# Layer 0's opening of a two-layer decoder trunk: where its subtractions run, how wide its w_ada multiply-adds are, and how many column blocks it begins

## The chip, the cores and the metric

The kernel runs on one core of a Trainium2 chip, with one launch. The metric is the device time of one execution in microseconds (us); lower is better. The core has five engines with a queue of their own each: TensorE (PE; its weight loads are listed apart as PEld), VectorE (DVE), ScalarE (ACT), GpSimd (POOL) and SyncE (SP), which here only issues transfers. An engine takes its instructions strictly in the order in which the program lists them, and waits on semaphores for the others. 16 DMA engines carry the transfers from HBM.

## What is computed

Two layers of a decoder. Each layer modulates its normalised input by vectors that come from c, projects it once into all heads and gates of three attention branches, merges them and adds to the residual. x has 256 rows of 2048 float32; w_in has 17944 columns per layer. What matters here is the start of layer 0:

```python
for l in range(2):
    mod = silu(c) @ w_ada[l] + b_ada[l]            # c: (1, 2048), w_ada[l]: (2048, 6144)
    shift, scale, gate = split(mod, 3)
    h = rmsnorm(x, norm_pre_g[l]) * (1 + scale) + shift
    a_q, a_k, a_v, a_z, ..., m_g = split(h @ w_in[l])   # w_in[l]: (2048, 17944)
    ...                                            # three attentions, w_branch, gates, w_out, residual
```

No column of h is known before the columns of shift and scale that belong to it. These need a full pass over 2048 rows of w_ada.

## The kernel before

**Products.** A float32 product is made of three products of a rounded type: a weight tile `raw` of 128x1024 (two k-tiles of 128 rows by 512 columns, 512 KB) is split by `split` (L265) into `wh`, a rounded copy made by ScalarE (L272), and `wl = raw - wh` (L273), made by VectorE unless an engine is passed. Likewise h is kept as `hh` and `hl`. `mm3` (L276) then runs `hh*wh`, `hh*wl`, `hl*wh` (L277 to L279). Below, a **unit** is one such weight tile: 2 k-tiles x 2 halves of 128 rows of x x 3 products = 12 matmuls of 512 columns, one cast and one subtraction. A column block of w_in (512 columns) has 8 units, over the 16 k-tiles of h.

**The body of the kernel** is `run_jobs` (L359): a list of jobs, one for each column block, unit after unit. Casts and subtractions run three units ahead (`L_CAST`), and loads four tiles ahead. Attention steps, evacuations (`sc.urgent`, one each tick) and the background multiply-adds of the next modulation vectors (`ada_steps`, L434) are woven between the units.

**Layer 0's opening** is `start_layer0` (L899). Nothing of h is there at the start, so it computes shift and scale in pieces and begins column blocks of w_in with those k-tiles of h that are ready:

- w_ada's columns for shift and scale are taken in 8 chunks of 2 k-tiles (256 columns of shift and 256 of scale). A chunk needs all 2048 rows: 8 tiles of 512 KB, which are loaded in two transfers each. For each tile VectorE runs two multiply-adds (`madd`, L238: L240 the first one, L242 the others) of 128x512 into two accumulators.
- When a chunk is complete, `colsums` (L938) adds the two accumulators (L939), lets TensorE sum over the partitions (`colsum`, L246, behind the transposes of x, L516), finishes the columns (L251, L253) and writes these two k-tiles of hh and hl (L525 on VectorE, L527 and L533 on ScalarE, L534 on VectorE). It is queued one item after the chunk's last tile (`CLAG`).
- Between a chunk's w_ada tiles lie units of w_in, spread evenly (`seq`). `PLAN` says which: the blocks 0 to 3 (`LO`), 4 to 7 (`HI`) and block 8, each in segments of one to three units. In all there are 59 units in the opening. Their subtraction is passed to GpSimd (`split(w, NW, nc.gpsimd)`).
- A unit's matmuls are queued 3 items after it (`MLAG`). A segment holds two of the four PSUM banks; 6 items after its last unit (`SPILL`) it is stored by ScalarE (L965, a block's first segment) or added by VectorE into the block's partial result (L967).
- Raw tiles have 7 buffers (`RAW_BUFS`), wh and wl 4 each (`W_BUFS`). Transfers are issued by SP in the order of `seq`, 6 tiles ahead. x (two transfers of 1 MB) is issued ahead of all w_ada.
- x is normalised by ScalarE (`norm_x`, L501: L506, L510) ahead of its first cast.

After the opening the blocks begun in it are finished as ordinary jobs over their remaining k-tiles, the rest is added to the partial result (L1034). The jobs run in the order of layer 0's program: branch A's q, k, v, z (first half), four blocks of the merge gate, branch A's second half, and so on. In the kernel before, the merge gate blocks are `LO`, branch A's first four are `HI`, and block 8 is the first of branch A's second half.

Of the kernel before, what the change touches and what calls it, by code (L numbers as in the profile page):

```python
# [11 lines left out]
F32 = mybir.dt.float32  # L12
# [5 lines left out]
P = 128  # L18
# [65 lines left out]
def tiles(r, k0, k1):  # L84
    return [(i, k0, k1) for i in r]


LO, HI = range(4), range(4, 8)
PLAN = [tiles(LO, 0, 1), tiles(HI, 0, 2) + [(8, 0, 2)], tiles(LO, 1, 3), tiles(HI, 2, 4) + [(8, 2, 4)], tiles(LO, 3, 5), tiles(HI, 4, 6),
        tiles(LO, 5, 7) + [(8, 4, 7)]]  # L90
RAW_BUFS = 7
# [4 lines left out]
def body(ctx, tc, a, out):  # L96
# [51 lines left out]
    for f in vec_loads(0, nc.scalar):  # L148
        f()
    for t in range(NT):  # L150
        nc.sync.dma_start(xs[:, t], x_dram[0][t])

# [746 lines left out]
    def start_layer0(hh, hl, w_in, cols, parts, plan, mcols, S_):  # L899
        wv = a["w_ada"][0].rearrange("(k p) n -> p k n", p=P)  # L900
        CW = 2 * P
        NP = KD // 2
        seq = []
        done_k = [0] * len(cols)
        for p in range(NP):
            ws = [(i, k) for i, ks in plan[p] for k in ks]
            assert all(k < p for _, k in ws)
# [6 lines left out]
        raws, banks, accs = {}, {}, {}  # L914
        events = {}
        state = [0]

        def load_next():
            n = state[0]
            if n < len(seq):  # L920
                kind, x, y = seq[n]
                r = raw_tile()
                if kind == "a":
                    v = r.rearrange("p (k h n) -> p k h n", k=2, h=2)
                    for h in range(2):
                        c0 = h * D + x * CW
# [5 lines left out]
                raws[n] = r.rearrange("p (k n) -> p k n", k=2)  # L932
                state[0] += 1
# [3 lines left out]

        def colsums(p):  # L938
            nc.vector.tensor_add(accs[p][0], accs[p][0], accs[p][1])  # L939
            g = h_chunks(lambda k, t: xs[:, t, k * P:(k + 1) * P], p, lambda: (hh, hl), mcols[0], mcols[1])  # L940
            next(g)
            pb = pbank()
            for i in range(4):
                colsum(pb, i, [accs[p][0][:, i * P:(i + 1) * P]])
            for third in range(2):
                finish_cols(0, third, mcols[third], pb[:, 2 * third:2 * third + 2], 2 * p, 2)
            for _ in g:
                pass

# [23 lines left out]
        norm_x(xs, ssx, parts[7].rearrange("p t n -> p (t n)"))  # L973
        S_["lam"] = {}
# [6 lines left out]
        for n, (kind, x, y) in enumerate(seq):  # L981
            w = raws.pop(n)
            if kind == "a":
                if y == 0:
# [22 lines left out]
    def layer(l, S_, jobs):  # L1007
# [34 lines left out]
        if l == 0:  # L1042
            begin()
            first = [C_MG + j * NW for j in range(4)] + [C_AQ, C_AK, C_AV, C_AZ, C_AQ + NW, C_AK + NW]
            gpv = big.tile([P, D], F32, tag="gp", name="gpv", bufs=1).rearrange("p (j t n) -> p j t n", j=2, t=NT)
            qv = qk_tile().rearrange("p j s -> p (j s)").rearrange("p (t n) -> p t n", t=NT)
            ys = [big.tile([P, NT, NW], F32, tag=g, name="yv", bufs=2) for g in ("yh", "yl")]
            parts = [gpv[:, 0], gpv[:, 1], qv] + [pj() for _ in range(5)] + ys
            plan = [[]] + [[(i, list(range(k0, k1))) for i, k0, k1 in p] for p in PLAN]
# [449 lines left out]
```

## Time and profile before

| | us |
|---|---|
| time, median of 3 runs | 2314.87 (2314.47 to 2317.6) |
| span of the profiled execution | 2310.3 |
| TensorE busy in the span | 2223.7 |
| VectorE busy | 1561.6 |
| ScalarE busy | 1011.0 |
| GpSimd busy | 248.7 |

The profile gives for its one execution the span from the first to the last instruction; that is 4.6 us less than the median of the timed runs. Busy times are the time in which an engine has an instruction in work. Matmuls are pipelined, so a busy TensorE may still be waiting a little; the granted clock (PEclk, 1.00 is 2.4 GHz, 0.50 is 1.2 GHz) is read beside it. Rows of a timeline merge neighbouring instructions of one kind ("x4") and give start, length and, in brackets, the idle time ahead of them and what ended it.

### The profile page before, as it was taken

What the parts mean: (1) busy time and instruction counts of PE and PEld (TensorE: products, weight loads), DVE (VectorE), ACT (ScalarE), POOL (GpSimd) and SP (SyncE); (2) the same over time, 40 slices, a digit from 0 to 9 for tenths busy, and PEclk for the clock granted to TensorE, in tenths of its full rate; (3) what the DMA queues carried; (4) which work ended last, traced back from release to release, by engine and by line L of the source; (5) the groups of instructions that cost most, each with busy time, mean ns of one, the idle gap of its engine ahead of it and who ended that gap; (6) DMA issues with size and microseconds to landing.
All of it is one profiled execution on the core that took longest, in us unless ns stands there. A gap on an engine that the chain in (4) does not pass through costs nothing.

```text
span 2310.3 us, 30428 instructions
## 1 busy us (share of the span) xinstructions
PE 2223.7 (96%) x11474; PEld 1891.4 (82%) x11474; DVE 1561.6 (68%) x1991; ACT 1011.0 (44%) x1429; POOL 248.7 (11%) x170
## 2 busy tenths in 40 slices
PE   5787899999999999999999999999999999999998
PEld 3666788999988889888877888889998888987886
DVE  7999897767677757677556655565556564666664
ACT  4332355444444435454445444444444443445443
POOL 4765400000001100001110000000000010000010
PEclk9988999999999999999999999999999999999999
DMA  9877777887878877667656677667666776655663
GB/s 312 272 235 252 243 238 233 253 260 219 248 229 263 262 230 253 197 199 246 219 168 192 190 217 220 192 189 214 183 204 180 218 219 199 206 175 164 195 232 121
DMA packets 317603, 504.76 MB, mean 218 GB/s; under 512 B 16921, under 2 KB 124177, under 8 KB 317201
## 3 DMA queue, kind: packets, MB, share of 16 engines
q1 hardware_dynamic: 317232, 502.54, 69.8%
q8 instruction: 90, 1.47, 0.3%
q14 instruction: 57, 0.46, 0.1%
q10 hardware_dynamic: 224, 0.29, 0.0%
HBM read 498.56 MB, written 4.19 MB: 218 GB/s over the span
## 4 chain that ended last, share of the span: by engine, by line
PE 87%; DVE 7%; issue 3%; DMA 1%; ACT 1%; SPq 0%; POOL 0%; DVEq 0%; ACTq 0%; POOLq 0%
PE mbank L277 22%; PE mbank L279 22%; PE mbank L278 22%; DVE wk L242 5%; PE mbank L422 4%; PE mbank L423 4%; PE mbank L424 4%; DMA raw<-w_ada 1%; PE pbank L756 1%; DVE wk L240 1%; PE pbank L628 1%; PE pbank L878 1%; PE pbank L851 1%; PE pbank L583 1%; PE pbank L246 0%
## 5 line engine op out<-in xcount | busy, mean ns | idle before, releaser
L273 DVE TENSOR_TENSOR wl<-raw,wh 128x1024 fp32r<-128x1024 f32 (+1 forms) x668 | 809.8, 1217 | 586.7 <-ACT wh L272 582.6
L272 ACT CAST wh<-raw 128x1024 fp32r<-128x1024 f32 (+1 forms) x730 | 751.1, 1033 | 762.5 <-PE mbank L279 539.3
L277 PE MATMUL mbank<-wh,hh 128*128 128x512 f32 (+1 forms) x1912 | 764.9, 400 | 17.8 <-DVE gpv L967 6.9
L278 PE MATMUL mbank<-wl,hh 128*128 128x512 f32 (+1 forms) x1912 | 740.5, 387 | 7.1 <-POOL wl L273 6.7
L279 PE MATMUL mbank<-wh,hl 128*128 128x512 f32 (+1 forms) x1912 | 739.8, 387 | 0.0
L277 PEld LDWEIGHTS mbank<-wh,hh 128*128 128x128 f32 x1912 | 364.6, 191 | 93.6 <-issue 14.8
L278 PEld LDWEIGHTS mbank<-wl,hh 128*128 128x128 f32 x1912 | 364.8, 191 | 80.8 <-POOL wl L273 9.3
L279 PEld LDWEIGHTS mbank<-wh,hl 128*128 128x128 f32 x1912 | 363.6, 190 | 75.2 <-DVE hl L534 0.9
L422 PE MATMUL mbank<-hh,wh 128*128 128x256 f32 x768 | 220.2, 287 | 0.0
L424 PE MATMUL mbank<-hh,wl 128*128 128x256 f32 x768 | 217.3, 283 | 0.0
L423 PE MATMUL mbank<-hl,wh 128*128 128x256 f32 x768 | 217.2, 283 | 0.0
L242 DVE SCALAR_TENSOR_TENSOR acc<-raw,cT,acc 128x512 f32<-128x512 f32 x240 | 185.6, 773 | 5.9 <-DMA raw<-w_ada 1.4
L273 POOL TENSOR_TENSOR wl<-raw,wh 128x1024 fp32r<-128x1024 f32 x62 | 161.9, 2630 | 94.5 <-ACT wh L272 57.1
L242 DVE SCALAR_TENSOR_TENSOR wk<-raw,cT,wk 128x512 f32<-128x512 f32 x112 | 167.8, 1557 | 1.9 <-DMA raw<-w_ada 1.9
L277 PE MATMUL mbank<-wh,yh 128*128 128x512 f32 x384 | 150.6, 392 | 0.0
L279 PE MATMUL mbank<-wh,yl 128*128 128x512 f32 x384 | 149.6, 390 | 0.0
L278 PE MATMUL mbank<-wl,yh 128*128 128x512 f32 x384 | 149.5, 389 | 0.0
L423 PEld LDWEIGHTS mbank<-hl,wh 128*128 128x128 f32 x768 | 147.3, 192 | 0.5
L422 PEld LDWEIGHTS mbank<-hh,wh 128*128 128x128 f32 x768 | 147.2, 192 | 0.5
L424 PEld LDWEIGHTS mbank<-hh,wl 128*128 128x128 f32 x768 | 147.2, 192 | 0.0
L1153 POOL TENSOR_TENSOR merged<-merged,pj 128x512 f32<-128x512 f32 x32 | 50.9, 1611 | 522.2 <-DVE pj L1151 522.2
L277 PE MATMUL mbank<-wh,mh 128*128 128x512 f32 x240 | 94.0, 392 | 0.0
(238 smaller groups left out, 1855.6 us busy)
## 6 DMA issues: line engine op xcount, KB each, us to landing
raw<-w_in SPq DMA_DIRECT2D x544, 512.0 KB, 4.5
raw<-w_ada SPq DMA_DIRECT2D x128, 512.0 KB, 4.6
raw<-w_branch SPq DMA_DIRECT2D x96, 512.0 KB, 5.0
raw<-w_ada SPq DMA_DIRECT2D x128, 256.0 KB, 5.1
raw<-w_out SPq DMA_DIRECT2D x64, 512.0 KB, 4.6
raw<-w_in SPq DMA_DIRECT2D x32, 268.0 KB, 4.0
raw<-cmp_w_k SPq DMA_DIRECT2D x8, 512.0 KB, 4.4
raw<-cmp_w_v SPq DMA_DIRECT2D x8, 512.0 KB, 3.9
```

What stands on the lines that cost most here:

```text
L240: nc.vector.tensor_scalar(acc, w, cT[:, k:k + 1], None, op0=OP.mult)
L242: nc.vector.scalar_tensor_tensor(acc, w, cT[:, k:k + 1], acc, op0=OP.mult, op1=OP.add)
L272: nc.scalar.copy(wh[:, :, 0:n], src)
L273: (eng or nc.vector).tensor_tensor(wl[:, :, 0:n], src, wh[:, :, 0:n].bitcast(F32), op=OP.subtract)
L277: nc.tensor.matmul(o, hi, wh, start=first, stop=False)
L278: nc.tensor.matmul(o, hi, wl, start=False, stop=False)
L279: nc.tensor.matmul(o, lo, wh, start=False, stop=last)
L422: nc.tensor.matmul(o, wh[:, kk, cs], hi, start=(k == j.k0), stop=False)
L423: nc.tensor.matmul(o, wh[:, kk, cs], lo, start=False, stop=False)
L424: nc.tensor.matmul(o, wl[:, kk, cs], hi, start=False, stop=(k == j.nk - 1))
L583: nc.tensor.transpose(pb[:, j * P:(j + 1) * P], x[:, t, j * P:(j + 1) * P], ident)
L1153: nc.gpsimd.tensor_tensor(dst, dst, sg[:, t], op=OP.add)
```

## The change

Five things change, all in the opening of layer 0.

1. The subtraction of a unit in the opening is made by VectorE (`split` without an engine), not by GpSimd.
2. w_ada is taken in chunks of 2, 2, 4, 4 and 4 k-tiles instead of eight of 2. In a chunk of 4 a tile holds one row tile of 512 + 512 columns, in one transfer, and one multiply-add of 128x1024 takes it, into an accumulator of 128x1024. In a chunk of 2, two of 128x512 as before.
3. A chunk of 4 has eight column sums instead of four, and its second pair of k-tiles of h (`whole`) is written one item after the first.
4. 12 blocks are begun instead of 9, all up to unit 6 of 8: 72 units in all. Branch A's eight blocks and the four of the merge gate are finished as jobs of 2 units. The segments are of one or two units.
5. x is issued behind w_ada's first tile (first half) and third tile (second half).

```diff
-LO, HI = range(4), range(4, 8)
-PLAN = [tiles(LO, 0, 1), tiles(HI, 0, 2) + [(8, 0, 2)], tiles(LO, 1, 3), tiles(HI, 2, 4) + [(8, 2, 4)], tiles(LO, 3, 5), tiles(HI, 4, 6),
-        tiles(LO, 5, 7) + [(8, 4, 7)]]
+CHUNKS = ((0, 2), (2, 2), (4, 4), (8, 4), (12, 4))
+LO, HI = range(7), range(7, 12)
+PLAN = [tiles(LO, 0, 1), tiles(HI, 0, 2) + tiles(LO, 1, 2), tiles(range(12), 2, 4), tiles(range(12), 4, 6)]
...
-    for t in range(NT):
-        nc.sync.dma_start(xs[:, t], x_dram[0][t])
...
-        wv = a["w_ada"][0].rearrange("(k p) n -> p k n", p=P)
...
+        wv = a["w_ada"][0].rearrange("(k p) (h n) -> p k h n", p=P, n=D)
...
-            for u in range(NP):
-                lo, hi = [-(-i * len(ws) // NP) for i in (u, u + 1)]
+            na = KD * nk // 4
+            for u in range(na):
+                lo, hi = [-(-i * len(ws) // na) for i in (u, u + 1)]
                 seq.extend(("w",) + x for x in ws[lo:hi])
-                seq.append(("a", p, u))
+                seq.append(("a", c, u))
...
-                    v = r.rearrange("p (k h n) -> p k h n", k=2, h=2)
-                    for h in range(2):
-                        c0 = h * D + x * CW
-                        nc.sync.dma_start(v[:, :, h], wv[:, 2 * y:2 * y + 2, c0:c0 + CW])
+                    k0, nk = CHUNKS[x]
+                    ku = 4 // nk
+                    v = r.rearrange("p (k h n) -> p k h n", k=ku, h=2)
+                    for k in range(ku):
+                        nc.sync.dma_start(v[:, k], wv[:, ku * y + k, 0:2, k0 * P:(k0 + nk) * P])
...
-        def colsums(p):
-            nc.vector.tensor_add(accs[p][0], accs[p][0], accs[p][1])
...
+        def colsums(c):
+            k0, nk = CHUNKS[c]
+            acc = accs[c]
+            if nk == 2:
+                nc.vector.tensor_add(acc[:, 0:NW], acc[:, 0:NW], acc[:, NW:2 * NW])
+            g = piece(k0 // 2)
             next(g)
             pb = pbank()
-            for i in range(4):
-                colsum(pb, i, [accs[p][0][:, i * P:(i + 1) * P]])
+            for i in range(2 * nk):
+                colsum(pb, i, [acc[:, i * P:(i + 1) * P]])
...
+        def whole(k2):
+            for _ in piece(k2):
                 pass
...
-        for _ in range(RAW_BUFS - 1):
+        for n in range(RAW_BUFS - 1):
             load_next()
+            if n in (0, 2):
+                nc.sync.dma_start(xs[:, n // 2], x_dram[0][n // 2])
...
                 if y == 0:
-                    accs[x] = [wk(NW), wk(NW)]
-                for k in range(2):
-                    madd(accs[x][k], w[:, k], 2 * y + k, y == 0)
+                    accs[x] = qk_tile().rearrange("p j s -> p (j s)")
+                acc = accs[x]
+                if nk == 2:
+                    for k in range(2):
+                        sl = slice(k * NW, (k + 1) * NW)
+                        madd(acc[:, sl], r[:, sl], 2 * y + k, y == 0)
+                else:
+                    madd(acc, r, y, y == 0)
...
-                if y == NP - 1:
-                    at(n + (CLAG if x else 1), lambda p=x: colsums(p))
+                if y == KD * nk // 4 - 1:
+                    at(n + (CLAG if x else 1), lambda c=x: colsums(c))
+                    for j in range(1, nk // 2):
+                        at(n + CLAG + j, lambda k2=k0 // 2 + j: whole(k2))
             else:
-                wh, wl = split(w, NW, nc.gpsimd)
+                wh, wl = split(r.rearrange("p (k n) -> p k n", k=2), NW)
...
-            first = [C_MG + j * NW for j in range(4)] + [C_AQ, C_AK, C_AV, C_AZ, C_AQ + NW, C_AK + NW]
+            first = [C_AQ, C_AK, C_AV, C_AZ] + [C_MG + j * NW for j in range(4)] + \
+                [C_AQ + NW, C_AK + NW, C_AV + NW, C_AZ + NW]
```

The rest of the diff names where the 12 partial results and the scratch of `norm_x` lie.

## Rows read from the trace of the kernel before

**Rows 1.** Windows, TensorE alone: stretch, length, busy (instructions), granted clock, DMA share, GB/s.

```profile
0.00:254.40 254.40, 185.50 (x738) 0.91 0.81 264
254.40:2310.30 2055.90, 2038.23 (x10736) 1.00 0.69 213
```

**Rows 2.** Windows, line 277 alone: PE, PEld busy (instructions), clock, DMA.

```profile
25.80:254.40 228.60, 93.29 (x216) 45.05 (x217) 0.90 0.79 254
```

**Rows 3.** Windows: PE, PEld, DVE, ACT, POOL busy (instructions), clock, DMA share, GB/s.

```profile
25.80:254.40 228.60, 181.70 (x724) 143.50 (x725) 212.48 (x187) 74.81 (x89) 151.89 (x59) 0.90 0.79 254
268.30:324.80 56.50, 56.50 (x263) 46.96 (x263) 53.35 (x80) 27.67 (x44) 3.87 (x2) 1.00 0.72 227
271.10:284.70 13.60, 13.60 (x61) 11.23 (x61) 13.43 (x21) 6.21 (x7) 0.00 (x0) 1.00 0.71 225
8.00:25.00 17.00, 3.24 (x12) 2.46 (x12) 12.16 (x23) 8.20 (x10) 4.64 (x7) 1.00 1.08 384
20.00:40.00 20.00, 12.60 (x46) 9.94 (x46) 17.17 (x21) 7.21 (x10) 10.16 (x4) 0.99 0.97 333
200.00:220.00 20.00, 16.83 (x74) 13.11 (x73) 20.00 (x18) 5.25 (x5) 13.72 (x6) 1.00 0.91 297
```

**Rows 4.** Timeline of TensorE: start, us, operation, [idle before <- what ended it].

```profile
25.84 0.80 PE L277 MATMUL mbank<-wh,hh 128*128 128x512 f32 x1 [1.86 <-ACT hh L533]
...
254.40 0.77 PE L277 MATMUL mbank<-wh,hh 128*128 128x512 f32 x1 [5.44 <-DVE gpv L967]
```

**Rows 5.** Waits of TensorE from 25.8 to 254.5: us, times, longest.

```profile
PE pbank L246 <- DVE wk L939: 20.4, 6, 5.3
PE mbank L277 <- DVE gpv L967: 6.9, 3, 5.4
```

**Rows 6.** VectorE's groups: from 48 to 69 us, up to 256 us, after it.

```profile
L242 DVE SCALAR_TENSOR_TENSOR wk<-raw,cT,wk 128x512 f32<-128x512 f32 x6 | 16.9, 2881 | 0.0
...
L242 DVE SCALAR_TENSOR_TENSOR wk<-raw,cT,wk 128x512 f32<-128x512 f32 x108 | 165.0, 1587 | 1.9 <-DMA raw<-w_ada 1.9
...
L273 DVE TENSOR_TENSOR wl<-raw,wh 128x1024 fp32r<-128x1024 f32 x636 | 786.9, 1242 | 564.3 <-ACT wh L272 562.3
L242 DVE SCALAR_TENSOR_TENSOR acc<-raw,cT,acc 128x512 f32<-128x512 f32 x240 | 185.6, 773 | 5.9 <-DMA raw<-w_ada 1.4
```

**Rows 7.** Timelines of GpSimd and VectorE, same columns as rows 4.

```profile
49.73 18.92 POOL L273 TENSOR_TENSOR wl<-raw,wh 128x1024 fp32r<-128x1024 f32 x7 [5.17 <-DMA raw<-w_ada]
14.63 6.71 DVE L242 SCALAR_TENSOR_TENSOR wk<-raw,cT,wk 128x512 f32<-128x512 f32 x10
121.16 13.30 POOL L273 TENSOR_TENSOR wl<-raw,wh 128x1024 fp32r<-128x1024 f32 x5 [8.38 <-PE mbank L279]
129.36 1.27 DVE L967 TENSOR_TENSOR pj<-pj,mbank 128x512 f32<-128x512 f32 x2
272.07 4.62 DVE L273 TENSOR_TENSOR wl<-raw,wh 128x1024 fp32r<-128x1024 f32 x4
2295.18 2.48 DVE L1350 SCALAR_TENSOR_TENSOR oo<-oo,rstd,pj 128x1024 f32<-128x1024 f32 x2
```

**Rows 8.** Timeline of VectorE at the close of a chunk.

```profile
21.37 0.69 DVE L939 TENSOR_TENSOR wk<-wk 128x512 f32<-128x512 f32 x1
24.02 0.23 DVE L251 TENSOR_TENSOR col<-pbank,vc 128x2 f32<-128x2 f32 x2 [1.96 <-PE pbank L246]
25.82 0.69 DVE L534 TENSOR_TENSOR hl<-wk,hh 128x512 fp32r<-128x512 f32 x1 [0.76 <-ACT hh L533]
...
268.50 0.23 DVE L251 TENSOR_TENSOR col<-pbank,vc 128x2 f32<-128x2 f32 x2 [3.71 <-PE pbank L246]
```

**Rows 9.** ScalarE's timeline: x's second half, its scaling, the first cast.

```profile
8.85 1.06 ACT L506 ACTIVATE pj<-xs 128x1024 f32<-128x1024 f32 x1 [0.20 <-DMA xs<-x]
...
11.08 3.88 ACT L510 ACTIVATE xs<-xs,rstd 128x2048 f32<-128x2048 f32 x2
21.00 1.04 ACT L272 CAST wh<-raw 128x1024 fp32r<-128x1024 f32 x1 [6.03 <-DMA raw<-w_in]
```

More of the change, by code (lines that the diff above doesn't have):

```diff
@@ L899, in start_layer0 @@
     def start_layer0(hh, hl, w_in, cols, parts, plan, mcols, S_):
-        wv = a["w_ada"][0].rearrange("(k p) n -> p k n", p=P)
-        CW = 2 * P
-        NP = KD // 2
+        wv = a["w_ada"][0].rearrange("(k p) (h n) -> p k h n", p=P, n=D)
         seq = []
[L904 to L907, printed above, removed]
-            for u in range(NP):
-                lo, hi = [-(-i * len(ws) // NP) for i in (u, u + 1)]
+        for c, (k0, nk) in enumerate(CHUNKS):
+            ws = [(i, k) for i, ks in plan[c] for k in ks]
+            assert all(2 * k < k0 for _, k in ws)
+            na = KD * nk // 4
+            for u in range(na):
+                lo, hi = [-(-i * len(ws) // na) for i in (u, u + 1)]
                 seq.extend(("w",) + x for x in ws[lo:hi])
-                seq.append(("a", p, u))
+                seq.append(("a", c, u))
         ends = {(i, ks[-1]) for pl in plan for i, ks in pl}
         begins = {(i, ks[0]) for pl in plan for i, ks in pl}
-        raws, banks, accs = {}, {}, {}
+        raws, banks, accs, bank_of = {}, {}, {}, {}
+        done_k = [0] * len(cols)
         events = {}
@@ L931, in load_next @@
                                       w_in[:, 2 * y:2 * y + 2, c0:c0 + NW])
-                raws[n] = r.rearrange("p (k n) -> p k n", k=2)
+                raws[n] = r
                 state[0] += 1
@@ L936, in at, with piece @@
             events.setdefault(s, []).append(f)
-        def colsums(p):
-            nc.vector.tensor_add(accs[p][0], accs[p][0], accs[p][1])
-            g = h_chunks(lambda k, t: xs[:, t, k * P:(k + 1) * P], p, lambda: (hh, hl), mcols[0], mcols[1])
+        def piece(k2):
+            return h_chunks(lambda k, t: xs[:, t, k * P:(k + 1) * P], k2, lambda: (hh, hl), mcols[0], mcols[1])
+        def colsums(c):
[4 more added lines that the diff above has]
+            g = piece(k0 // 2)
             next(g)
             pb = pbank()
-            for i in range(4):
-                colsum(pb, i, [accs[p][0][:, i * P:(i + 1) * P]])
+            for i in range(2 * nk):
+                colsum(pb, i, [acc[:, i * P:(i + 1) * P]])
             for third in range(2):
-                finish_cols(0, third, mcols[third], pb[:, 2 * third:2 * third + 2], 2 * p, 2)
+                finish_cols(0, third, mcols[third], pb[:, nk * third:nk * (third + 1)], k0, nk)
             for _ in g:
+                pass
+        def whole(k2):
+            for _ in piece(k2):
                 pass
@@ L967, in spill @@
                     nc.vector.tensor_add(parts[i][:, t], parts[i][:, t], banks[i][t])
-        for _ in range(RAW_BUFS - 1):
+        for n in range(RAW_BUFS - 1):
             load_next()
+            if n in (0, 2):
+                nc.sync.dma_start(xs[:, n // 2], x_dram[0][n // 2])
         silu_c()
         ssx = sm.tile([P, 2 * NT], F32, tag="ssx", name="ssx", bufs=1)
-        norm_x(xs, ssx, parts[7].rearrange("p t n -> p (t n)"))
+        norm_x(xs, ssx, parts[3].rearrange("p t n -> p (t n)"))
         S_["lam"] = {}
@@ L1043, in layer @@
             begin()
-            first = [C_MG + j * NW for j in range(4)] + [C_AQ, C_AK, C_AV, C_AZ, C_AQ + NW, C_AK + NW]
+            first = [C_AQ, C_AK, C_AV, C_AZ] + [C_MG + j * NW for j in range(4)] + \
+                [C_AQ + NW, C_AK + NW, C_AV + NW, C_AZ + NW]
             gpv = big.tile([P, D], F32, tag="gp", name="gpv", bufs=1).rearrange("p (j t n) -> p j t n", j=2, t=NT)
             qv = qk_tile().rearrange("p j s -> p (j s)").rearrange("p (t n) -> p t n", t=NT)
-            ys = [big.tile([P, NT, NW], F32, tag=g, name="yv", bufs=2) for g in ("yh", "yl")]
-            parts = [gpv[:, 0], gpv[:, 1], qv] + [pj() for _ in range(5)] + ys
+            ys = [big.tile([P, NT, NW], F32, tag=g, name="yv", bufs=2) for g in ("yh", "yl", "yh", "yl")]
+            pjs = [pj() for _ in range(5)]
+            parts = ys[0:2] + pjs[0:2] + [gpv[:, 0], gpv[:, 1], qv, pjs[2]] + ys[2:4] + pjs[3:5]
             plan = [[]] + [[(i, list(range(k0, k1))) for i, k0, k1 in p] for p in PLAN]
```

3 lines of the change are left out of this document (2 added, 1 removed).

## The prediction

> **What bounds the kernel now.** I first split the span where TensorE stops waiting. After 254.4 us it is busy for 2038 of 2056 us at the full clock: there TensorE is the bound, and work taken out of its list shortens the kernel by that work's length. Before 254.4 us it is busy for 185 us at a mean granted clock of 0.91 [rows 1]. So the opening is the only place with much to win, and two numbers matter: the time at which TensorE begins to run without a pause, and how many units it has done by then.
>
> A unit's price is a matmul's pitch in a full stretch: 13.60 us with 61 matmuls in work, one left over from before, is 60 pitches of 0.2267 us [rows 3], so 12 of them are **2.72 us**. Up to 254.4 us line 277 runs 216 times [rows 2], four to a unit: 54 units, 147 us at full clock. So **107.5 us** of the first 254.4 are lost for units.
>
> What loses them is VectorE. From 25.8 to 254.4 us it is busy for 212 of 229 us, GpSimd for 152, transfers at 254 GB/s [rows 3]. A multiply-add of 128x512 costs 1587 ns here and 773 ns later, and the rows show when: from 48 to 69 us six take 2881 ns each [rows 6], beside seven GpSimd subtractions in 18.9 us, 2.70 each; ten with GpSimd idle take 6.7 us [rows 7], while transfers run at 384 GB/s [rows 3]. So it is GpSimd that holds them, not the transfers. An add that reads a PSUM bank is not held: two take 1.27 us in the middle of five GpSimd subtractions [rows 7]. TensorE's waits name the same chain: 20.4 us for the last multiply-adds of a chunk, 6.9 us for additions queued behind them [rows 5].
>
> **The change part by part.** I count what each engine has to do until the 72 units are through; the last of the three sums sets the new mark E.
>
> *Start.* The bytes ahead of the first w_in tile are the same, only x comes later, so its cast still starts at 21.0 [rows 9]. The second half of x now has 1.57 MB of w_ada more ahead of it, at 384 GB/s 4.1 us; ScalarE's scaling, which ended at 14.96, ends at 19.1 [rows 3, 9]. Nothing, therefore: the cast's own tile hides it with 1.9 us to spare; if that is gone, the excess comes in full. The earlier first multiply-add is worth nothing either, since the chunk's last tile has the same bytes ahead. But the first subtraction now stands on VectorE ahead of the chunk's close: cast until 22.1, subtraction until 23.3, then the addition that began at 21.37 [rows 8]. That is a **loss of 1.9 us**: first matmul at 27.7 instead of 25.84 [rows 4], VectorE free at 28.4 instead of 26.5.
>
> *VectorE from 28.4 on.* 71 subtractions: four in 4.62 us, a last one of 1.22, so pitch 1.13 us [rows 7]: 80. 16 narrow multiply-adds at 0.67 [rows 7]: 10.5. 48 wide ones: none is in the trace on this tile; bounds are a subtraction's pitch, 1.13, and two narrow ones, 1.34; the same operation at this width on other tiles takes 2.48 for two [rows 7], so I take 1.22: 58. Additions of PSUM banks, 31 segments that are not a block's first, two each at 0.60 [rows 7]: 37. Seven pairs of k-tiles of h and four closes, about 1.2 + 0.4 [rows 8]: 10. Small side steps: 3. Together 199, ending at 227; with a wait for the column sums and ScalarE at each close (2.0 to 3.7, and 0.76 [rows 8]), 4 x 3.5, at **241**.
>
> The rows show the next subtraction starting 1.13 us after one that lasts 1.22, so nothing lies between two of them. The Trainium skill has a rule that speaks against putting more on this engine: VectorE: DVE Perf Modes, section "The DRAIN you can't avoid", says that behind every operation the pipe is flushed for about the operation's length less 266 ns before the next one starts. By that estimate a subtraction would take 2.17 us (rival V); the rows contradict it for this very instruction.
>
> *Transfers.* 136 tiles of 0.524 MB, x 2.1, constants 0.8: 74.2 MB. The stretches with a full queue give 384 and 333 GB/s, a late one 297 [rows 3]: 193, 223 or 250 us. I take 333, the longest of the full ones: **223**, hidden by the others.
>
> *TensorE.* From 27.7: 72 units, 196 us. Closes (transposes, column sums, twice as many in a wide chunk): 9. The first unit at half clock: 2.5. And a bubble at each of four closes. VectorE stands at the column sums, which are behind two or three queued units; once they are there it needs 2.5 us to the end of hl [rows 8], a subtraction 1.13 and a bank's addition 1.2 before the next segment has a bank: 4.8. TensorE has one unit (2.7) and the next piece's transposes (0.4) for that time: 1.7 short, and about as much at the next segment: 3. I take 3 a close, with 0 and 6 as bounds: 12. Sum **E = 248**, the largest of the three. ScalarE's 72 casts at 1.04 [rows 9] are 75 of these 220 us; it is no bound.
>
> *Gain in the opening.* Lost for units then: 248 - 196 = 52 instead of 107.5, a gain of **55.5**; one more close is inside than in the 254.4 us before, 1.
>
> *After the opening.* 12 jobs of 2 units follow, 24 units, 71 us with their transposes. VectorE's demand there: 24 subtractions, 27 us; 12 pairs of additions to the partial results, 14; and attention and background. These are what remains of the stretch 268.3 to 324.8, where VectorE is busy for 53.35 us beside 20 units [rows 3], when 20 subtractions and 9 pairs of additions, 33 us, are taken off: 20, or by the same rate 24 for 24 units, and up to 13 more as the second half's rotations and gate fall into it too. Together 65 to 78 of 71. Before, that stretch was nearly full too, but began with five units queued on TensorE; now it begins right behind the last chunk's close with one. I take 6 us, bounds 0 and 15.
>
> Sum: 55.5 + 1 - 6 = **50.5 us**. 2310.3 - 50.5 = 2259.8 for the span; the median of the timed runs lies 4.6 above the profiled span: **2264 us**.
>
> **The rivals.**
>
> *C, the clock stays low.* The opening ran at 0.90 [rows 3]: a fifth of the time at half clock. The four PSUM banks and the closes keep TensorE pausing after the change as well. If it stays at 0.90 over 220 us, E is 248 + 20, **2284**. Against: 196 of the 220 us are units, and in full stretches the clock is 1.00 [rows 3]. The Trainium skill, TensorE: Matmul & The Clock Gate, section "A second HAM failure mode: psum-queue depth-cycling", says that short pauses between groups of matmuls on cycling banks make the clock swing between its two levels, which is this rival.
>
> *D, the transfers become the bound.* If the queue gives the 297 GB/s of 200 to 220 us, the last tile lands at 250 and the close behind it (4.8) makes E 255: **2271**. For: a DMA share of 0.91 there. Against: buffers were then held by slow multiply-adds.
>
> *S, slower: additions of banks hold TensorE.* There are 31 with VectorE instead of 22. TensorE waited 5.4 us for one that stood behind multiply-adds [rows 4, 5]. Each us on each of the 31 costs 31 us; from 1.6 us the gain is gone, at 2.5 the time is **2341**. Against: a wait of that kind came three times, 6.9 us [rows 5], behind multiply-adds that GpSimd held; and a segment's addition is queued two items ahead of the matmuls that need its banks.
>
> *T, VectorE isn't relieved.* If the multiply-adds are slow for another reason, 48 wide ones at twice 1.59 [rows 6] add 94 us to 241, E is 335: **2351**. Against: the ten at 0.67 beside transfers at 384 GB/s [rows 3, 7].
>
> *V, VectorE pauses between its operations.* If each of its operations is followed by a pause of its own length less 0.27 us, VectorE's 199 become about 360 and E 400: **2416**. Against: the four subtractions in 4.62 us [rows 7]. This is the rule on the flush named above.
>
> **How the numbers follow.** The forecast with its own bounds (closes 0 to 6, jobs 0 to 15) runs from 2246 to 2285 and gets 0.72; C 0.10, D 0.08, S 0.04, T 0.01, V 0.01, a result below 2246 (closes and jobs cost nothing and the wide operation is at its lower bound) 0.03, a near cancelling of all 0.01. The range 2246 to 2288 takes in the forecast, C and D. Measurement tells about 0.2% (4.6 us): faster 0.93, same 0.01, slower 0.06.
>
> **What would show it.** In the profile after: multiply-adds of 128x1024 near 1.25 us and subtractions on VectorE near 1.22 in the opening, GpSimd nearly idle; first matmul near 27.7; 288 runs of line 277 by the mark, which is near 248; clock near 0.97 in the opening; TensorE's remaining pauses at the four closes, 3 us each; some 6 us of pauses in the 70 us behind the mark, for subtractions or banks. Wrong it would be if subtractions on VectorE wait for their casts behind spills and the mark lies beyond 270, or if the jobs of two units starve by more than 15 us.

## The result, and the profile after

The changed kernel takes 2277.03 us (median, 2276.32 to 2278.07) against 2314.67 for the kernel before: a ratio of 0.984 with a 95% interval of 0.9826 to 0.9854, 37.6 us less. The forecast was 2264 us, 50.5 less. The sign, the place and the cause were right; 13 us of the gain are missing. The profiled execution has a span of 2274.5 us, 35.8 under the one before.

Windows of the kernel after, columns as in [rows 1] (TensorE alone), then line 275 alone (the unit's first matmul, line 277 before) as in [rows 2], then all engines as in [rows 3]. The mark, the point from which TensorE hardly pauses, is now at 262.59:

```profile
0.00:262.59 262.59, 221.76 (x980) 0.97 0.87 300
262.59:2274.50 2011.91, 1988.80 (x10495) 0.99 0.68 212
...
30.70:262.59 231.89, 118.28 (x293) 56.71 (x293) 0.97 0.86 295
...
30.70:262.59 231.89, 217.96 (x966) 178.21 (x966) 199.06 (x234) 98.15 (x116) 2.48 (x2) 0.97 0.86 295
```

293 runs of line 275 are 73.25 units, 199.2 us of full-clock work, so 63.4 of the first 262.59 us are lost for units, where it was 107.5. The opening gained 44.1 us, not 55.5. GpSimd, busy for 152 us of the old opening, does nothing in the new one but 2.5 us of side steps.

VectorE's groups from 20 to 262 us of the kernel after (operation and count, then busy us, mean ns, idle before), which answer to [rows 6, 7]:

```profile
L271 DVE TENSOR_TENSOR wl<-raw,wh 128x1024 fp32r<-128x1024 f32 x74 | 89.4, 1217 | 10.5 <-ACT wh L270 10.5
L240 DVE SCALAR_TENSOR_TENSOR qkT<-raw,cT,qkT 128x1024 f32<-128x1024 f32 x45 | 57.6, 1280 | 0.0
L975 DVE TENSOR_TENSOR pj<-pj,mbank 128x512 f32<-128x512 f32 x24 | 15.3, 678 | 0.0
```

The wide multiply-add, priced from other tiles at 1.22 us, lasts 1.28. VectorE is busy for 199.06 us of the stretch, where the prediction's list came to 199.

TensorE's timeline after (columns as in [rows 4]; of four rows between 93 and 105 us and two near 190 the first stands):

```profile
30.70 0.80 PE L275 MATMUL mbank<-wh,hh 128*128 128x512 f32 x1 [1.82 <-ACT hh L531]
55.88 0.80 PE L275 MATMUL mbank<-wh,hh 128*128 128x512 f32 x1 [3.25 <-ACT gpv L973]
93.62 0.50 PE L275 MATMUL mbank<-wh,hh 128*128 128x512 f32 x1 [1.71 <-DVE yv L975]
...
116.70 0.76 PE L275 MATMUL mbank<-wh,hh 128*128 128x512 f32 x1 [3.99 <-DVE gpv L975]
189.02 0.47 PE L275 MATMUL mbank<-wh,hh 128*128 128x512 f32 x1 [1.42 <-DVE pj L975]
...
262.59 0.50 PE L276 MATMUL mbank<-wl,hh 128*128 128x512 f32 x1 [1.52 <-DVE wl L271]
313.24 0.30 PE L626 MATMUL pbank<-ident,wk 128*128 128x128 f32 x1 [2.36 <-DVE wk L659]
395.55 0.78 PE L685 MATMUL pbank<-ident,wk 128*128 128x128 f32 x2 [2.50 <-DVE wk L678]
```

Before, TensorE waited 20.4 us for the last multiply-adds of its chunks [rows 5]; that wait is gone. What is left are pauses for spilled banks (lines 973 and 975), one for a subtraction at the mark, and two new ones well behind the mark, in front of attention's transposes, where the old kernel paused for 0.35 us in all between 254.4 and 480.

### The profile page after: what moved, and what is told of

Its sections match the earlier page's. It is cut to its first block, busy times and chain, and to the rows that moved or that the text cites. A ratio compares the mean times of both kernels' runs of the same rounds, so it can differ in the third digit from the quotient of the medians.

```text
span 2274.5 us, 30350 instructions
## 1 busy us (share of the span) xinstructions
PE 2210.6 (97%) x11474; PEld 1883.7 (83%) x11474; DVE 1528.2 (67%) x2011; ACT 1012.8 (45%) x1431; POOL 96.2 (4%) x111
## 4 chain that ended last, share of the span: by engine, by line
PE 94%; DVE 3%; issue 1%; ACT 1%; DMA 1%; POOL 0%; SPq 0%; DVEq 0%; ACTq 0%; POOLq 0%
PE mbank L275 24%; PE mbank L277 24%; PE mbank L276 24%; PE mbank L421 4%; PE mbank L422 4%; PE mbank L420 4%; PE pbank L754 1%; PE pbank L626 1%; DVE wl L271 1%; PE pbank L876 1%; PE pbank L849 1%; PE pbank L581 1%; DMA raw<-w_ada 0%; ACT wh L270 0%; PE pbank L244 0%
## 5 line engine op out<-in xcount | busy, mean ns | idle before, releaser
L271 DVE TENSOR_TENSOR wl<-raw,wh 128x1024 fp32r<-128x1024 f32 (+1 forms) x727 | 877.8, 1212 | 585.8 <-ACT wh L270 578.2
L277 PE MATMUL mbank<-wh,ml 128*128 128x512 f32 x240 | 93.4, 389 | 0.0
L276 PE MATMUL mbank<-wl,mh 128*128 128x512 f32 x240 | 93.4, 389 | 0.0
L277 PEld LDWEIGHTS mbank<-wh,yl 128*128 128x128 f32 x384 | 72.2, 188 | 15.4
```

Of the source, the lines that this page charges most:

```text
L271: (eng or nc.vector).tensor_tensor(wl[:, :, 0:n], src, wh[:, :, 0:n].bitcast(F32), op=OP.subtract)
L276: nc.tensor.matmul(o, hi, wl, start=False, stop=False)
L277: nc.tensor.matmul(o, lo, wh, start=False, stop=last)
```

## The experiments

My theory: GpSimd's leaving the subtractions carries the gain; the missing 13 us lie in the later start, in pauses beside the third chunk, and in the jobs behind the mark. The rivals: the blocks begun, or the width of the multiply-adds, carry it. Medians and intervals against the kernel before:

| kernel | median us | ratio, 95% | span | mark | span less mark |
|---|---|---|---|---|---|
| after | 2277.03 | 0.9826 to 0.9854 | 2274.5 | 262.59 | 2011.9 |
| before, subtractions on VectorE | 2269.62 | 0.9795 to 0.9824 | 2268.9 | | |
| after, subtractions on GpSimd | 2291.63 | 0.9885 to 0.9918 | 2290.0 | 279.11 | 2010.9 |
| after, 9 blocks | 2276.82 | 0.9825 to 0.9854 | 2275.4 | | |
| after, narrow multiply-adds | 2276.98 | 0.9825 to 0.9855 | 2275.6 | 264.61 | 2011.0 |
| after, x first | 2274.56 | 0.9812 to 0.9839 | 2272.7 | 260.84 | 2011.9 |
| after, first close early | 2274.64 | 0.9816 to 0.9843 | 2273.2 | 261.39 | 2011.8 |
| after, segments alternating | 2273.63 | 0.9812 to 0.9839 | 2270.9 | 259.27 | 2011.6 |
| after, background late | 2282.92 | 0.9852 to 0.9879 | 2281.1 | 262.45 | 2018.7 |
| the three edits | 2270.59 | 0.9796 to 0.9823 | 2269.0 | 257.15 | 2011.9 |
| the three edits, six units fewer | 2272.53 | 0.9798 to 0.9825 | 2270.5 | | |
| before, VectorE, first close early | 2269.83 | 0.9793 to 0.982 | 2267.8 | | |
| the three edits, output projection later | 2268.01 | 0.9788 to 0.9815 | 2265.4 | 259.37 | 2006.0 |

The mark is the same event in every row that has one (the subtraction behind the last chunk's close, after the same 73.25 units). The last column is what follows it.

### One part alone: the subtractions on VectorE

```diff
-                wh, wl = split(w, NW, nc.gpsimd)
+                wh, wl = split(w, NW)
```

> The kernel before with one edit: the opening's subtractions on VectorE instead of GpSimd; its 59 units, 9 column blocks, narrow multiply-adds and x ahead of w_ada stay. Theory (the change gains mainly because GpSimd leaves the subtractions): the 59 units are done by about 245 us of the trace instead of 54 by 254.4, so some 245 - 59 x 2.72 = 85 us are lost in the opening instead of 107.5, and the time is 2285 to 2297 us; the 128x512 multiply-adds fall from 1587 ns to under 900 ns. Rival (the gain comes from more blocks begun or from wider multiply-adds): within 6 us of 2314.7.

Measured: 2269.62 us, 7.4 less than the whole change. VectorE's groups from 20 to 245 us, then TensorE's waits from 28 to 240 us (us, times, longest), then line 277's window and TensorE's window behind the opening:

```profile
L273 DVE TENSOR_TENSOR wl<-raw,wh 128x1024 fp32r<-128x1024 f32 x67 | 81.1, 1218 | 4.0 <-ACT wh L272 4.0
L242 DVE SCALAR_TENSOR_TENSOR wk<-raw,cT,wk 128x512 f32<-128x512 f32 x102 | 71.4, 743 | 0.0
...
PE pbank L246 <- DVE wk L939: 15.1, 7, 3.8
...
28.66:229.00 200.34, 96.39 (x235) 0.95 0.92 308
...
300.00:420.00 120.00, 120.00 (x644) 1.00 0.78 246
```

The multiply-adds fall from 1587 ns [rows 6] to 743. So the first theory holds, and more than I expected: this one line is worth 45 us, and the rest of the change, put on top of it, loses 7.4.

The edit takes away two things at once: the slow multiply-adds, and GpSimd's own slow subtractions. The kernel before had these waits of TensorE too from 25.8 to 254.5 us, beside those of [rows 5]:

```profile
PE mbank L278 <- POOL wl L273: 6.7, 5, 1.9
PE mbank L277 <- DVE pj L967: 3.6, 3, 2.0
```

With 2.2 us more for line 967, TensorE waited 33.1 us for VectorE's multiply-adds and additions and 6.7 for GpSimd's subtractions themselves. By the trace the first route is the larger one; no run separates the two.

The rows also say where the rest of the change loses. At 229 us its 58.75 units are through and 69.2 us are lost, 5.8 more than in the kernel after: the rest of the change does serve the opening. But from 300 to 420 us this kernel never pauses, while the kernel after, in the same window, does:

```profile
300.00:420.00 120.00, 113.97 (x605) 0.97 0.67 212
```

6.0 us idle and 3% of the clock, 3.6 us: 9.6 us behind the mark against 5.8 ahead of it. That is 3.8 of the spans' 5.6 us; the other 1.8 are not located.

### The rest alone: GpSimd back

```diff
-                wh, wl = split(r.rearrange("p (k n) -> p k n", k=2), NW)
+                wh, wl = split(r.rearrange("p (k n) -> p k n", k=2), NW, nc.gpsimd)
```

> The changed kernel with one edit: the opening's subtractions back on GpSimd; 12 blocks, wide multiply-adds, w_ada ahead of x stay. Theory (GpSimd is what held the opening): GpSimd needs about 2.9 us a unit, 73 x 2.9 = 212 us, and slows VectorE's multiply-adds, so most of the gain goes: 2300 to 2325 us, multiply-adds of 128x1024 at 1.9 us or more instead of 1.28. Rival (width or blocks carry the gain): at most 2287 us, and multiply-adds near 1.28 us.

Measured: 2291.63 us, between the two. The groups of VectorE and of GpSimd in the opening, then the mark on TensorE's timeline:

```profile
L240 DVE SCALAR_TENSOR_TENSOR qkT<-raw,cT,qkT 128x1024 f32<-128x1024 f32 x45 | 113.0, 2512 | 13.2 <-DMA raw<-w_ada 12.9
L975 DVE TENSOR_TENSOR pj<-pj,mbank 128x512 f32<-128x512 f32 x24 | 15.6, 678 | 4.0 <-PE mbank L277 4.0
...
L271 POOL TENSOR_TENSOR wl<-raw,wh 128x1024 fp32r<-128x1024 f32 x72 | 212.4, 2983 | 34.1 <-ACT wh L270 34.1
...
279.11 0.50 PE L276 MATMUL mbank<-wl,hh 128*128 128x512 f32 x1 [1.53 <-DVE wl L271]
```

The multiply-adds take 2512 ns instead of 1280 and the mark comes 16.5 us later, which is the whole difference of the spans (15.5) and 1 more. GpSimd's 2.98 us a unit are more than TensorE's 2.72, and TensorE waits for it 16 times, 7.0 us in all. My 2300 to 2325 was too long by 8 us at least: the rest of the change gains 23 us where GpSimd subtracts. A reason may be that a wide multiply-add loses 1.23 us to GpSimd and two narrow ones 1.63 [rows 6]; no run tests this. The gains don't add: 45 and 23 alone, 37.6 together.

The additions that read a PSUM bank stay at 678 ns in both kernels, as in [rows 7], while the multiply-adds, which have two inputs in SBUF, double. The Trainium skill, SBUF — State Buffer, section "Who interferes with whom", says that VectorE meets GpSimd's reads only where it has two inputs in SBUF or a two-port mode; for these operations the traces agree. A chunk's first multiply-add, with one tensor input, is slowed too (line 240: 480 ns with the subtractions on VectorE, 1295 in the kernel before), which could be the two-port case; no run shows the mode.

### Fewer blocks, narrower multiply-adds

```diff
-LO, HI = range(7), range(7, 12)
+LO, HI = range(7), range(7, 9)
-... tiles(range(12), 2, 4), tiles(range(12), 4, 6)]
+... tiles(range(9), 2, 4), tiles(range(9), 4, 6)]
```

> The changed kernel with only 9 of the 12 column blocks begun in the opening: 54 units instead of 73; everything else stays. Theory (the opening is bound by transfers of w_ada and w_in and by VectorE, and each unit carries its own bytes and its own subtraction): fewer units end the opening sooner, about 54 x 2.72 + 63 = 210 us, and cost as much TensorE time later; the time is 2270 to 2286 us, within 9 us of the changed kernel's 2277. Rival (the number of blocks begun carries the gain): the opening doesn't get shorter by as much as 19 x 2.72 = 52 us, and the time is 2295 us or more.

```diff
-                    madd(acc, r, y, y == 0)
+                    for h in range(2):
+                        sl = slice(h * NW, (h + 1) * NW)
+                        madd(acc[:, sl], r[:, sl], y, y == 0)
```

> The changed kernel with each 128x1024 multiply-add made as two of 128x512 (48 instructions of 1.28 us become 96 of about 0.745 us, 71.5 instead of 61.4 us). Theory (width only trims VectorE's load by 10 us of which part is hidden): 2 to 7 us longer, 2279 to 2284. Rival (width carries the gain): 15 us longer or more.

Measured: 2276.82 and 2276.98 us, neither to be told from 2277.03. So neither rival carries the gain. (The size of the chunks was not varied by itself.) With 9 blocks the opening ends at 218.13 instead of 262.59 after 55.25 units: 67.8 us lost, 4.4 more than with 12. Behind it no pause is left at the place of 395 us. Its mark, and TensorE's window behind it:

```profile
218.13 0.50 PE L276 MATMUL mbank<-wl,hh 128*128 128x512 f32 x1 [1.36 <-DVE wl L271]
...
300.00:420.00 120.00, 120.00 (x639) 1.00 0.77 246
```

Three blocks more save 4.4 us in the opening and cost 3.5 of them behind it, by the spans. The narrow multiply-adds are some 10 us more work for VectorE (90 of 743 ns and 6 first ones of about 480 in place of 45 of 1280 and 3 of 746) and move the mark by 2.0 us; 0.9 of them come back behind it, and my 2279 to 2284 was not reached: width is hidden nearly in full.

### The start: x first, and the first close early

```diff
+        for t in range(NT):
+            nc.sync.dma_start(xs[:, t], x_dram[0][t])
         for n in range(RAW_BUFS - 1):
             load_next()
-            if n in (0, 2):
-                nc.sync.dma_start(xs[:, n // 2], x_dram[0][n // 2])
```

> The changed kernel with x's two transfers issued ahead of the first six tiles of w_ada, as in the kernel before. Theory (the order of the transfers at the start costs the changed kernel some 2 to 3 us): the first matmul of the w_in units comes at 27.5 to 28.7 us instead of 30.7, and the time falls by 1.5 to 3 us, to about 2274.5. Rival (the later start is hidden: VectorE's chunks or the transfers set the end of the opening whatever the start): the first matmul comes earlier, but the time stays within 1 us of 2277.

```diff
-                    at(n + (CLAG if x else 1), lambda c=x: colsums(c))
+                    at(n + (CLAG if x else 0), lambda c=x: colsums(c))
```

> The changed kernel with the closing add of chunk 0 queued on VectorE ahead of the first subtraction instead of behind it. Theory: the column sums of chunk 0 start 1.2 to 3 us earlier (at 24 to 26 us instead of 27.0), the first matmul of the w_in units at 28 to 29.5 us instead of 30.7, and the time falls by 1 to 3 us. Rival (as for x: the start is hidden): within 1 us of 2277.

Measured: 2274.56 and 2274.64 us, 2.5 and 2.4 less. The intervals of the ratios overlap with that of the kernel after, though every execution of the two is shorter than its shortest (2275.36 and 2275.24 us at most, against 2276.32). The marks lie 1.75 and 1.2 us earlier, with 2011.8 to 2011.9 us behind them in all three. Rows of the kernel after: the issue of the first w_in tile on SyncE's queue, that queue's waits up to 20 us, the first cast, the first subtraction and the closing add behind it. The next two rows are the first cast and the first matmul with x first, and the last two TensorE's window from 2 to 20 us, before and after, for its last columns, DMA share and GB/s:

```profile
18.03 0.37 SPq L928 DMA_DIRECT2D raw<-w_in  x1
...
SPq L925 <- DMA xs<-x: 4.0, 2, 2.0
...
24.06 1.04 ACT L270 CAST wh<-raw 128x1024 fp32r<-128x1024 f32 x1 [1.45 <-DMA raw<-w_in]
25.13 1.22 DVE L271 TENSOR_TENSOR wl<-raw,wh 128x1024 fp32r<-128x1024 f32 x1 [1.54 <-ACT wh L270]
26.28 0.68 DVE L943 TENSOR_TENSOR qkT<-qkT 128x512 f32<-128x512 f32 x1
...
21.41 1.04 ACT L270 CAST wh<-raw 128x1024 fp32r<-128x1024 f32 x1 [5.53 <-DMA raw<-w_in]
28.05 0.80 PE L275 MATMUL mbank<-wh,hh 128*128 128x512 f32 x1 [1.82 <-ACT hh L531]
...
2.00:20.00 18.00, 1.93 (x6) 1.00 1.04 370
2.00:20.00 18.00, 0.56 (x2) 1.00 0.98 329
```

The cast at 24.06 is the step the prediction put at 21.0, unmoved. The issue of w_in's first tile comes at 18.03; with x first the cast is back at 21.41 and the first matmul at 28.05. The queue's 4.0 us of waits for x's transfers don't explain this alone, since it has 2.8 of them in the kernel before and 2.9 with x first. What differs is the rate: from 2 to 20 us the transfers run at 329 GB/s, against 370 before and 366 with x first. That is 0.7 MB less, or some 2 us at 370 GB/s. Why it is lower with x between the small transfers is open.

### Beside the third chunk: segments alternating

```diff
-        tiles(HI, 0, 2) + tiles(LO, 1, 2),
+        [t for h, lo in zip(((7,), (8,), (9,), (10,), (11,)), ((0,), (1, 2), (3,), (4, 5), (6,)))
+         for t in tiles(h, 0, 2) + tiles(lo, 1, 2)],
```

> The changed kernel with another order of the same 17 units beside the third chunk: the five two-unit segments (blocks 7 to 11) alternate with the seven one-unit segments (blocks 0 to 6) instead of standing ahead of them. Theory (one-unit segments in a row cost VectorE 1.20 + 1.13 + 1.20 = 3.5 us a unit against TensorE's 2.72, so TensorE pauses between 93 and 117 us and runs at half clock after it): the five pauses there shrink from 7.4 us to under 4, and the time falls by 3 to 6 us. Rival (VectorE and the transfers are busy in this stretch in any order, and the pauses only move): within 1.5 us of 2277.

Measured: 2273.63 us, 3.4 less, mark 3.3 earlier. VectorE in the kernel after, beside the one-unit segments, and TensorE's pauses between 92 and 116 us with the alternating order:

```profile
92.89 1.27 DVE L975 TENSOR_TENSOR yv<-yv,mbank 128x512 f32<-128x512 f32 x2
94.09 1.27 DVE L240 SCALAR_TENSOR_TENSOR qkT<-raw,cT,qkT 128x1024 f32<-128x1024 f32 x1
95.28 1.21 DVE L271 TENSOR_TENSOR wl<-raw,wh 128x1024 fp32r<-128x1024 f32 x1
96.42 1.27 DVE L975 TENSOR_TENSOR yv<-yv,mbank 128x512 f32<-128x512 f32 x2
...
102.44 0.50 PE L276 MATMUL mbank<-wh,hh 128*128 128x512 f32 x1 [2.33 <-DVE gpv L976]
115.99 0.50 PE L276 MATMUL mbank<-wh,hh 128*128 128x512 f32 x1 [2.40 <-ACT pj L974]
```

From 92.89 to 96.42 VectorE makes one unit's round in 3.53 us without a gap, against TensorE's 2.72: a bank is added up after every unit instead of after every second one. In the new order the five pauses of 7.4 us between 93 and 117 are two of 4.7, but two others (1.76 and 0.32) appear near 80 and 86. So the pauses moved more than they shrank: TensorE's idle time up to the mark falls only from 13.9 to 13.4 us. Most of the 3.3 us is the clock. After the old pause of 3.99 us the matmuls follow at 0.43 instead of 0.23 us from 116.70 to 122.4; after the new one of 2.40 the granted clock is 1.00. That is worth 2.4 us, and another 0.4 is an earlier first matmul, which the edit doesn't touch.

### Behind the mark: background multiply-adds later

```diff
         def tick_bg(self):
+            if self.hold:
+                self.hold -= 1
+                return
...
+            sc.hold = 40 if l == 0 else 0
-            sc.bg_rate = len(sc.bg) * BG_STEPS / (ticks - BG_SPARE)
+            sc.bg_rate = len(sc.bg) * BG_STEPS / (ticks - BG_SPARE - sc.hold)
```

> The changed kernel with layer 0's background multiply-adds held back for the first 40 steps of the jobs behind the opening and made at a higher rate afterwards; the work is the same. Theory (behind the opening twelve short jobs end within some 65 us, and their additions, subtractions and transposes meet the background multiply-adds on VectorE, so TensorE pauses at 313 and 395 us and runs at half clock after each): the pauses of 2.36 and 2.50 us vanish, with the clock at 1.00 in 300:320 and 380:400, and the time falls by 4 to 8 us, to 2269 to 2273. Rival (the pauses come from the chain of a job's own steps, not from VectorE's load): within 1.5 us of 2277.

Measured: 2282.92 us, 5.9 more. TensorE's timeline, its window, and its longest wait from 400 to 900 us:

```profile
311.06 0.30 PE L630 MATMUL pbank<-ident,wk 128*128 128x128 f32 x1 [0.32 <-DVE wk L663]
391.37 1.99 PE L689 MATMUL pbank<-ident,wk 128*128 128x128 f32 x8 [2.48 <-DVE wk L682]
...
300.00:320.00 20.00, 18.62 (x85) 1.00 0.37 116
...
PE mbank L276 <- DVE wl L271: 3.1, 2, 2.0
```

My theory fell. It is right for the pause at 313 us, which shrinks from 2.36 to 0.32 with the clock at 1.00: VectorE's load. It is wrong for the one at 395, which stays at 2.48. And what was held back returns at a higher rate and makes TensorE wait from 400 to 900 us, where it had hardly waited; 6.8 us more behind the mark.

### Three edits at once, and two ways to lose the pause at 395 us

x first, the early first close and the alternating segments together, by the diffs above:

> The changed kernel with three edits of the earlier runs at once: x issued ahead of w_ada (alone 2.5 us), the close of chunk 0 ahead of the first subtraction (alone 2.4 us) and the third chunk's segments alternating (alone 3.4 us). Theory (two starts on one chain share part of their gain, the pauses at 93 to 117 us are apart from them): first matmul of the units at about 27 us, 2269 to 2272 us in all. Rival (all three are one slack, found at the close of the third chunk): 2273 us or more.

Measured: 2270.59 us, as the theory had it. First matmul 26.31, mark 5.4 us earlier than in the kernel after, 2011.9 us behind it as ever. The gains alone, 2.5, 2.4 and 3.4, become 6.4. Its pauses behind the mark are untouched:

```profile
307.82 0.30 PE L627 MATMUL pbank<-ident,wk 128*128 128x128 f32 x1 [2.38 <-DVE wk L660]
...
390.12 1.20 PE L686 MATMUL pbank<-ident,wk 128*128 128x128 f32 x4 [2.50 <-DVE wk L679]
```

The new theory for the second of them: attention's steps go forward with the steps of the jobs. In the kernel before, 45 job steps lie between the launch of the first heads and the output projection that waits for all of them (by the plans: 4 in the merge blocks, 1 and 24 in the second half's four, 8 and 8 in the two blocks behind them); in the kernel after they are 8, 8, 8 and 8, so 32, as the blocks begun in the opening took the rest out of that list. With 9 blocks they are 50, and no pause was there. With 32 the heads' last steps are left over at the wait and made in a row, with no matmuls between them. Two edits on top of the three test it: fewer units begun (38 steps), and the output projection put behind two more jobs (40 steps):

```diff
-        ..., tiles(range(12), 4, 6)]
+        ..., tiles(range(9), 4, 6)]
```

> The same three edits, and the last chunk continues 9 of the 12 blocks, so that blocks 9 to 11 go into the jobs with four units left instead of two: 67 units in the opening and 6 more job steps behind it. Theory (the pauses at 313 and 395 us come from the jobs behind the opening having become too short: the branch's follow-up work goes forward by job steps, and twelve short jobs give it too few; with 9 blocks begun the pause at 395 was not there): the pause at 395 us shrinks below 1 us and the one at 313 us below 1.5 us, and the time is 3 to 6 us under the kernel with the three edits. Rival (fewer units begun cost as much in the opening): within 1.5 us of it.

```diff
+        if l != 0:
             yA()
         proj_Td(C_SQ, "cq0")
+        if l == 0:
+            yA()
```

> The kernel with the three edits (2270.6 us), and in layer 0 the output projection of the first branch (whose first job waits for its attention heads) comes behind the two jobs of C_SQ instead of ahead of them: 8 more job steps between the launch of the last heads and the wait, nothing in the opening touched. Theory (the pause near 390 us is the heads' last steps made in a row because the begun blocks left too few job steps, 32 instead of the kernel before's 45 between the first launch and the wait): the pause of 2.50 us at 390.1 vanishes and the clock there stays at 1.00, the pause at 307.8 stays, and the time falls by 3 to 5 us, to 2266 to 2268. Rival (the pause is only put off, to the later job or to the second branch's wait): another pause of 1.5 us or more behind 390 us, and the time within 1.5 us of 2270.6.

The first gives 2272.53 us, no gain (four of its five executions lie between 2272.28 and 2273.27, one at 2265.99). TensorE's pauses and its window:

```profile
295.02 0.30 PE L627 MATMUL pbank<-ident,wk 128*128 128x128 f32 x1 [1.68 <-DVE wk L660]
...
362.35 0.30 PE L627 MATMUL pbank<-ident,wk 128*128 128x128 f32 x1 [1.53 <-DVE wk L660]
...
300.00:420.00 120.00, 118.08 (x634) 1.00 0.73 234
```

The pause at 390 is gone, as expected, and the stretch is 4.2 us fuller; but the first pause, now at 295, is 1.68 and not under 1.5, one of 1.53 us stands at 362, and the opening gives the gain back: with six units fewer its mark is at 245.05 after 67.25 units, so 62.1 us are lost where the three edits alone lost 57.9. So the cause stood, and the price of the remedy was left out of the expectation.

The second gives 2268.01 us, 2.6 less (2265.17 to 2269.05 against 2269.96 to 2271.84). Its mark, and the window in which the pause had been:

```profile
259.37 0.50 PE L277 MATMUL mbank<-wl,hh 128*128 128x512 f32 x1 [1.52 <-DVE wl L272]
...
380.00:400.00 20.00, 20.00 (x158) 1.00 0.92 292
```

The pause is gone and none takes its place (the one of 2.37 at 310.01 stays, as expected): 2006.0 us behind the mark instead of 2011.9, 5.9 less. In the profiled execution the opening, which the edit doesn't touch, ended 2.2 us later, with a clock of 0.88 from 100 to 114 us where the three edits alone had 1.00. The times by themselves don't show the gain: the kernel before, run beside each, has medians of 2313.59 and 2315.68 us, 2.1 apart. The traces do: the same pause vanishes with 38, 40 and 50 steps and stands with 32. So that pause comes from the list of job steps. This kernel's time is the shortest of all that were run, but its interval overlaps with that of the one-line edit.

### The one-line edit with an early first close

```diff
-                    at(n + (CLAG if x else 1), lambda p=x: colsums(p))
+                    at(n + (CLAG if x else 0), lambda p=x: colsums(p))
```

> The kernel before with its subtractions on VectorE (2269.6 us) and the closing add of chunk 0 ahead of the first subtraction. Theory (as in the changed kernel, where it brought 2.4 us): the first matmul of the units at 26.5 to 27.5 us instead of 28.66, 1 to 2.5 us less: about 2268. Rival (the seven closes behind it set the opening whatever the start): within 0.7 us of 2269.6.

Measured: 2269.83 us against 2269.62, so the rival holds. The first matmul comes 1.6 us earlier, yet the close of the sixth chunk is where it was (163.68 with the late first close):

```profile
27.05 0.79 PE L277 MATMUL mbank<-wh,hh 128*128 128x512 f32 x1 [2.77 <-ACT wh L272]
...
163.42 1.82 PE L246 MATMUL pbank<-ones,wk 128*128 128x1 f32 x8 [3.80 <-DVE wk L939]
```

With narrow chunks TensorE waits at the closes for the chunk's own multiply-adds (seven times, 15.1 us, with the late first close; six times, 13.3, with the early one), and 1.6 us of start drown in that. In the changed kernel, with four closes and more units between them, the same edit reached the end. Whether a start counts depends on what stands behind it.

## Why the prediction came out as it did

**Right: what bounded the kernel.** GpSimd's subtractions held VectorE's multiply-adds, and for the larger part through these the opening. The one-line edit shows it alone (1587 to 743 ns, 45 us), and putting GpSimd back shows it the other way. Rival T is out. V is out: the timeline beside the third chunk has a multiply-add of 1.27 us start 1.20 after the additions and a subtraction 1.19 after the multiply-add. The estimate by the Trainium skill's rule on the flush (VectorE: DVE Perf Modes, "The DRAIN you can't avoid") is contradicted by these rows too; the same section adds that a next operation which is not held starts earlier, and the prediction left that out. S is out: 9.2 us of waits for the additions in the opening. The prediction set 6.9 us in three waits against this rival and missed the others of line 967 (3.6 and 2.2); before, it was 12.7. D is out as a bound of the whole: 295 GB/s over the stretch, with stretches at 351 to 355 (20 to 40 and 60 to 80 us). In places the transfers still count: ScalarE's casts waited 13.3 us for their tiles.

**Right: the prices of VectorE.** 1.28 us where 1.22 was taken, 199 us in the sum.

**Wrong: the start, 3.0 us.** "Nothing, therefore: the cast's own tile hides it" failed. I counted bytes and took their rate as unchanged; with x between the small tiles the transfers ran at 329 GB/s from 2 to 20 us, and the tile was issued at 18.03, where the kernel before issued it at 14.97. The term for the subtraction ahead of the close, 1.9 us, was right (the early close gets 1.7 of it at the first matmul).

**Mis-sized: TensorE's row in the opening.** From the first matmul to the mark I had 23.5 us beside the units (closes 9, half clock 2.5, bubbles 12); measured are 231.89 - 199.2 = 32.7. Idle are 13.9, near the 12. Of these, 10.5 lie behind the four closes, whose column sums start at 51.7, 107.6, 182.4 and 252.8 us: 3.25, 3.99, 1.8 and 1.5, or 2.6 a close where I had 3. The other 3.4 lie beside the one-unit segments, which I hadn't priced. The clock of 0.97 over 231.89 us stands for 7, not 2.5, and the matmuls' pitch says 6.5: it is 0.43 instead of 0.23 us not only in the first unit, up to 33.4 us, but also from 55.88 to 60.7 and from 116.70 to 122.4, behind the two longest pauses. TensorE's window there:

```profile
116.70:125.00 8.30, 8.30 (x25) 0.66 0.79 245
```

That is rival C's mechanism at a third of its size. (The Trainium skill's rule on cycling banks, TensorE: Matmul & The Clock Gate, "A second HAM failure mode: psum-queue depth-cycling", agrees in kind: two of the nine pauses between the first matmul and the mark brought the clock down.) The remaining 11.8 are in the main the closes' matmuls, some 11 by their groups (column sums 6.5, transposes 4.2), where I had 9.

**Size right, place wrong: the jobs.** I charged 6 us within 0 to 15, in the 70 us behind the mark, for subtractions or banks; measured are 9.6 from 300 to 420, 9.3 by difference (44.1 + 1 - 35.8). That the sizes are so near is in part luck. One pause is VectorE's load, at the place I named (313, shrunk by the late background). The other, at 395, I hadn't seen: a list of job steps that paces attention, shortened by the blocks begun.

Sum: start 3.0, TensorE's row 9.2, rounding of the mark -0.8, jobs 3.3 more: 14.7 on the span (2274.5 against 2259.8), and 13 on the median, which lies 2.5 above this span and not 4.6. These 2 us are luck: in every other run on record a time lies 1.7 to 1.9 above its own execution's span, so by this estimate some 2.8 of the 4.6 came from a profiled execution of the kernel before that was shorter than its median.

**Not seen at all:** that most of the change beyond its one line would not pay. I priced the blocks' 18 units by what they save in the opening and not against the same opening without them; 9 blocks and 12 come out at the same time.

## What to carry to other kernels

Before pricing a bundle, price its strongest line alone: here the move of one operation off GpSimd was worth 45 us, and the bundle around it 37.6. Work drawn forward from a list that also paces other work leaves that other work without its cover, so count the steps left between each launch and its wait. And a pause of TensorE can cost more than its length: one of 2.5 us left the clock at 0.91 over 20 us, 1.8 more, and what follows the mark was 5.9 us shorter without it.

## What the runs showed of the hardware

- Against a multiply-add of VectorE with two inputs in SBUF, GpSimd's subtraction of 128x1024 lasts 2.98 us in the mean; the multiply-add goes from 743 to 1587 ns at 512 and from 1280 to 2512 at 1024. Additions with one input in PSUM stay at 678.
- The clock doesn't answer to a pause's length alone. In the kernel with the three edits pauses of 2.36 us at 100.34 and 2.40 at 113.89 left the granted clock at 1.00 (windows 100:114 and 114:140); 2.38 at 307.82 and 2.50 at 390.12 brought it to 0.91 over 20 us (300:320 and 380:400). TensorE's windows of that kernel:

```profile
114.00:140.00 26.00, 26.00 (x115) 1.00 0.92 310
300.00:320.00 20.00, 16.43 (x68) 0.91 0.57 175
```

  Ahead of the first two TensorE had paused not long before (1.85 us up to 77.42, then the 2.36 up to 100.34); from the mark at 257.15 to the third it had run without a break, and so it had ahead of the fourth from 315 us on. Why the same opening gave 0.88 over 100 to 114 us in another execution is open.
